# A layer norm over ragged sequences: the first tile's two halves loaded by two engines, the lengths behind one of them

## The chip, the core and the metric

The kernel runs on one core of a Trainium2 chip. A core has five engines with queues of their own: PE (matrix multiply), DVE (vector), ACT (scalar), POOL (GpSimd) and SP (SyncE, which here only issues transfers). SP, ACT and POOL can each start transfers between the main memory (HBM) and the on-chip memory; 16 DMA engines carry them out. The metric is the device time of one execution in microseconds. The kernel before takes 258.73 us (median of three runs, 258.59 to 258.74).

## The reference

```python
batch, max_seq, dim = (32, 512, 1024)
lengths = np.random.randint(64, max_seq, size=batch)
for b in range(batch):
    seq_len = lengths[b]
    x_b = x[b, :seq_len].copy()
    mean = np.mean(x_b, axis=-1, keepdims=True)
    var = np.var(x_b, axis=-1, keepdims=True)
    x_norm = (x_b - mean) / np.sqrt(var + eps)
    output[b, :seq_len] = x_norm * gamma + beta
```

`x` is 64 MB of float32. Rows past a sequence's length come out as zero. Each length is at least 64, so the first 64 rows of every sequence are valid for certain.

## The kernel before

**Tiles.** Four rows of 1024 make a unit of 16 KB; a tile is 128 units, one for each partition, 2 MB. Tiles 0 to 3 are static: they hold the first 64 rows of all 32 sequences, so their addresses do not depend on the lengths. The tiles after them hold the remaining valid rows, packed without holes. Which unit goes where is computed from the lengths: `un` (units in each sequence), `cum` (their running sum), and from these `idx_i`, one column of addresses for each later tile. Units past the lengths are written with zeros from a tile `zt`, 128 units at a time, at addresses `zidx`.

**Transfers.** POOL loads tiles 1 and up with indirect transfers (L556) into eight rotating buffers, stores finished tiles (L578 for tile 0, L585 for the others) and issues the zero stores (L592). Its queue is in program order: load tile 1; some constants; loads of tiles 2 and 3; then, after waiting for `idx_i` and reading the number of units into a register, loads of tiles 4 to 7; the memset of `zt` (L202); then tile after tile a store, a zero store and the load of the tile seven ahead. Tile 0 is loaded directly, without an index, in two halves of 1 MB (two rows for each partition, so 8 KB each), by SP (L531). The half h increments the semaphore `s_xs[h]`. ACT issues at its start the lengths (L519, `len64`, broadcast to all 128 partitions, 256 bytes each), gamma and beta (L520 and L521, into `row_f`).

**Work on a half tile.** The work is done in halves, k = 0, 1, 2, ... DVE takes statistics (L394, four instructions, and L399), ACT a square root (L421), DVE the reciprocal and a small product (L384, L385), ACT the normalisation into float16 (L405), DVE the product with gamma (L378), PE an identity matmul and a matmul that adds beta (L430, L436), and ACT writes the result back into the tile's buffer with a mask as its scale (L414). Then POOL stores the tile.

**Order.** A small scheduler writes each engine's instructions in a fixed order, and an instruction waits only for semaphores. On DVE the order in front is: constants; `lenf` (L231), which waits for the lengths; `rem_i`, `un`, `cum`, `q_f`; the index grid L258 to L267, which ends in `idx_i`; a cast of the identity (L365); and then the statistics of half 0, with this loop:

```python
for k in range(NH):
    if k >= 2:
        dve_mul(k - 2)
    if k >= 1:
        dve_smalls(k - 1)
    dve_stats(k)
    if k == 1:
        tok["maskst"] = mask_static()
```

`mask_static` holds the masks and store addresses of the static tiles, with the cast L294 among them. `zero_index` and `mask_all` follow at k = 3 and k = 5. On ACT the order in front is: its three transfer issues, a table load with a dummy square root (L219), `row_h` (L222, waits for gamma and beta), `gamma_h` (L228), then the square root of half 0. `load_dep(t)` gives the semaphore of a half's data: `s_xs[0]` and `s_xs[1]` for tile 0.

Of the kernel before, what the change touches and what calls it, by code (L numbers as in the profile page):

```python
# [11 lines left out]
P = 128  # L12
UR = 4
ST_ROWS = 64
# [52 lines left out]
def kernel(tc, x, lengths, gamma, beta, eps, out):  # L67
    nc = tc.nc
    B, T, D = x.shape
# [13 lines left out]
    s_len = tc.alloc_semaphore("s_len")  # L83
    s_row = tc.alloc_semaphore("s_row")
    s_xs = [tc.alloc_semaphore(f"s_xs{i}") for i in range(2)]
# [13 lines left out]
    with pool_cm as sb, psum_cm as psb:  # L99
        def st(shape, dt, name):  # L100
            return sb.tile(shape, dt, name=name)

        xt = [st([P, UR * D], FP32, f"x{i}") for i in range(R)]
        ht = [st([P, 2, D], FP16, f"h{i}") for i in range(RH)]
        zt = st([P, UR * D], mybir.dt.bfloat16, "zt")
        len64 = st([P, B], mybir.dt.int64, "len64")
# [71 lines left out]
        def iota(t, pattern, base=0, mult=0):  # L178
# [9 lines left out]
            out=sidx[:, :], in0=p4_i[:, 0:1].broadcast_to([P, NST]), scalar=float(U - S0), in1=sb_i[:, :],  # L188
# [9 lines left out]
            out=idn_f[:, :], in_=idn_f[:, :], compare_op=OP.not_equal, fill=1.0,  # L198
# [141 lines left out]
        def zero_index():  # L340
            n, _, p3 = grid(0, NZ)
            nd = cum[:, B - 1 : B]
            a = add("DVE", lambda: dve.scalar_tensor_tensor(
                out=cz[:, :], in0=cz_f[:, :], scalar=nd, in1=cum[:, :], op0=OP.add, op1=OP.subtract), [a_cz])
            add("DVE", lambda: dve.memset(w3[:, B - 1 : B], 0.0))
            b = add("DVE", lambda: dve.tensor_scalar(out=w3[:, 0 : B - 1], in0=un[:, 1:B], scalar1=float(S0),
                                                     scalar2=None, op0=OP.add))
            z = add("DVE", lambda: dve.scalar_tensor_tensor(
                out=zb[:, :], in0=un[:, 0:1], scalar=float(S0), in1=nd, op0=OP.add, op1=OP.subtract))
            c = add("DVE", lambda: dve.tensor_tensor(  # L350
                out=p3, in0=q_f[:, 0:NZ, None].broadcast_to([P, n, B]),
                in1=cz[:, None, :].broadcast_to([P, n, B]), op=OP.is_ge), [a])
            d = add("DVE", lambda: dve.tensor_tensor(
                out=p3, in0=p3, in1=w3[:, None, :].broadcast_to([P, n, B]), op=OP.mult), [c, b])
            l = add("DVE", lambda: dve.tensor_scalar(out=low[:, :], in0=q_f[:, 0:NZ], scalar1=nd, scalar2=65536.0,
                                                     op0=OP.is_lt, op1=OP.mult))
            e = add("DVE", lambda: dve.tensor_reduce(out=zidx_s[:, :], in_=p3, op=OP.add, axis=AX.X), [d])
            f = add("DVE", lambda: dve.scalar_tensor_tensor(
                out=zidx_f[:, :], in0=q_f[:, 0:NZ], scalar=zb[:, 0:1], in1=zidx_s[:, :], op0=OP.add, op1=OP.add), [e, z])
            return add("DVE", lambda: dve.tensor_tensor(out=zidx[:, :], in0=zidx_f[:, :], in1=low[:, :], op=OP.add),  # L360
                       [f, l])
# [99 lines left out]
        def emit_op(e, name, op):  # L461
            _, fn, waits, inc = op
            for key, val in waits:
                e.wait_ge(handles[key], val)
            ins = fn()
            if inc:
                ins.then_inc(sem[name], 1)

        def units_register(e, name):

            r = e.alloc_register(f"{name}_nd")
            e.wait_ge(sem["DVE"], d_tot[1])
            e.reg_load(r, tot_i[0:1, 0:1])
            return r
# [7 lines left out]
        def run_engine(e, name, block, setup=None):  # L482
            base = nc.cur_bb
            guards = []
            r = None
            if setup is not None:
                setup()
            for op in pr.ops[name]:
                if op[0] == "op":
                    emit_op(e, name, op)  # L490
                else:
                    k = op[1]
                    if k == 2 * NST - 1:
                        r = units_register(e, name)
                        tiles_register(e, r)
                    if k >= 2 * NST + 1 and k % 2 == 1 and k < NH - 1:
                        nxt = f"{name}_s{k + 1}"
                        e.br_lt(r, (k + 1) // 2, f"{name}_exit", nxt)
                        for g in guards:
                            g.__exit__(None, None, None)  # L500
                        guards = [nc.bb(nxt, parent=base)]
                        guards[0].__enter__()
            e.br(f"{name}_exit")
            for g in guards:
                g.__exit__(None, None, None)
            with nc.bb(f"{name}_exit", parent=base):
                e.br(block.end_bb)

        with tc.tile_critical():
            with nc.Block() as block:  # L510

                @block.vector
                def _(e):
                    run_engine(e, "DVE", block)

                @block.scalar
                def _(e):
                    def setup():
                        e.dma_start(out=len64[:, :], in_=lengths[None, :].to_broadcast([P, B])).then_inc(s_len, 16)  # L519
                        e.dma_start(out=row_f[:, 0:D], in_=gamma[None]).then_inc(s_row, 16)  # L520
                        e.dma_start(out=row_f[:, D : 2 * D], in_=beta[None]).then_inc(s_row, 16)  # L521
                    run_engine(e, "ACT", block, setup)
# [4 lines left out]

                @block.sync
                def _(e):
                    for h in range(2):  # L530
                        e.dma_start(out=xt[0][:, 2 * h * D : 2 * h * D + 2 * D],  # L531
                                    in_=x[4 * h : 4 * h + 4, 0:ST_ROWS].rearrange("b (p r) d -> p b (r d)", r=2)
                                    ).then_inc(s_xs[h], 16)
                    e.br(block.end_bb)

                @block.gpsimd
                def _(e):
# [59 lines left out]
                    for op in pr.ops["POOL"]:  # L597
                        if op[0] == "op":
                            emit_op(e, "POOL", op)
                            continue  # L600
                        t = op[1][1]
                        if t == 1:
                            wait(a_sidx)
                        if t == NST:
                            wait(d_idx)
                            rt = units_register(e, "POOL")
                            rb = e.alloc_register("POOL_rb")
                            e.reg_alu(rb, rt, 7, OP.arith_shift_right)
                            tiles_register(e, rt)
                        guarded_load(t)  # L610
# [65 lines left out]
```

## Time and profile before

| what | value |
|---|---|
| median of three runs | 258.73 us |
| the profiled execution | 258.48 us, its span 256.5 us |
| PE, DVE, ACT busy | 141.8, 178.5, 182.9 us |
| POOL busy | 62.2 us |
| HBM read, written | 41.98 MB, 69.21 MB |
| share of the 16 DMA engines: q0 (POOL) | 95.9% |
| the same: q1 (SP), q10 (ACT) | 2.2%, 0.1% |
| packets: q0, q1, q10 | 7632, 288, 148 |

The span runs from the first to the last instruction; the execution's time has some 2 us around it. A line of the timeline has the start and the duration in microseconds, the engine (SPq, ACTq: its queue, here issuing a transfer), the kernel's line, the operation, what is written and what is read, and in brackets how long the engine stood idle before it and what ended that. In the slices of the span each digit is a busy share in tenths. The trace also holds a record of each packet that a DMA engine moved: its start, its queue, its size and its duration.

### The profile page before, as it was taken

How to read it: one execution, taken by the hardware profiler on the slowest of the kernel's cores; microseconds unless marked ns; L12 is line 12 of the kernel's file. 1: busy time of each engine (PE TensorE's matmuls, PEld its weight loads, DVE VectorE, ACT ScalarE, POOL GpSimd, SP SyncE). 2: the span in 40 equal slices, each digit the busy share in tenths (PEclk: the TensorE clock that was granted, in tenths of full speed). 3: DMA queues.
4: the chain of work that ended last, by engine and by line, in shares of the span. 5: the costliest groups of instructions: out<-in, count | busy, mean ns of one | idle time of the engine just before them, and what ended most of it. 6: DMA issues, size and time to landing. Idle time of an engine off the chain costs nothing.

```text
span 256.5 us, 1586 instructions
## 1 busy us (share of the span) xinstructions
PE 141.8 (55%) x306; PEld 32.5 (13%) x306; DVE 178.5 (70%) x421; ACT 182.9 (71%) x198; POOL 62.2 (24%) x68
## 2 busy tenths in 40 slices
PE   0101908274966678668767786677677867820000
PEld 0000202021211111111111111111111111100000
DVE  3979697987688778877887888688868886820000
ACT  2440756758799989998999899989998999850000
POOL 5183021040523322302103402140307130320000
DMA  4999999999999999999999999999999999999980
GB/s 169 426 433 425 432 427 418 436 437 432 425 438 419 441 419 439 427 432 437 424 429 429 432 429 433 422 438 424 439 422 437 416 439 427 432 430 419 442 353 10
DMA packets 8083, 105.42 MB, mean 411 GB/s; under 512 B 1388, under 2 KB 1388, under 8 KB 1390
## 3 DMA queue, kind: packets, MB, share of 16 engines
q0 software_dynamic: 7632, 103.13, 95.9%
q1 hardware_dynamic: 288, 2.10, 2.2%
q8 instruction: 4, 0.07, 0.1%
q14 instruction: 11, 0.09, 0.1%
q10 hardware_dynamic: 148, 0.04, 0.1%
HBM read 41.98 MB, written 69.21 MB: 433 GB/s over the span
## 4 chain that ended last, share of the span: by engine, by line
DVE 35%; PE 28%; ACT 18%; DMA 6%; issue 3%; POOLq 1%; ACTq 1%; SPq 0%; DVEq 0%; POOL 0%
DVE stats_132 L394 18%; PE ps_149 L430 14%; PE ps_149 L436 14%; DMA x_61<-in_x_dram 6%; DVE h_69 L378 3%; DVE h_71 L378 3%; DVE h_70 L378 3%; ACT x_63 L414 3%; ACT x_62 L414 2%; ACT x_61 L414 2%; ACT x_67 L414 2%; ACT x_68 L414 2%; ACT x_66 L414 2%; ACT x_65 L414 2%; ACT x_64 L414 2%
## 5 line engine op out<-in xcount | busy, mean ns | idle before, releaser
L436 PE MATMUL ps_149<-row_h,ones_h 1*128 1x512 f16 x76 | 35.8, 622 | 0.0
L436 PE MATMUL ps_150<-row_h,ones_h 1*128 1x512 f16 x76 | 35.8, 622 | 0.0
L430 PE MATMUL ps_149<-h_69,idn_h 128*128 128x512 f16 x28 | 13.2, 628 | 25.7 <-DVE h_69 L378 25.7
L430 PE MATMUL ps_149<-h_71,idn_h 128*128 128x512 f16 x24 | 11.3, 628 | 15.3 <-DVE h_71 L378 15.3
L430 PE MATMUL ps_149<-h_70,idn_h 128*128 128x512 f16 x24 | 11.3, 627 | 13.7 <-DVE h_70 L378 13.7
L430 PE MATMUL ps_150<-h_70,idn_h 128*128 128x512 f16 x28 | 13.2, 628 | 7.0 <-DVE h_70 L378 7.0
L378 DVE TENSOR_TENSOR h_69<-h_69,gamma_h 128x2048 f16<-128x2048 f16 x13 | 15.5, 1195 | 0.7 <-DVE mv_136 L399 0.7
L592 POOL DMA_INDIRECT out_dram<-zt,zidx x14 | 14.5, 1033 | 5.3 <-issue 4.0
L378 DVE TENSOR_TENSOR h_70<-h_70,gamma_h 128x2048 f16<-128x2048 f16 x13 | 15.4, 1187 | 0.0
L430 PE MATMUL ps_150<-h_71,idn_h 128*128 128x512 f16 x24 | 11.3, 628 | 6.6 <-DVE h_71 L378 6.6
L430 PE MATMUL ps_150<-h_69,idn_h 128*128 128x512 f16 x24 | 11.3, 627 | 6.6 <-DVE h_69 L378 6.6
L378 DVE TENSOR_TENSOR h_71<-h_71,gamma_h 128x2048 f16<-128x2048 f16 x12 | 14.3, 1190 | 0.0
L436 PEld LDWEIGHTS ps_150<-row_h,ones_h 1*128 1x128 f16 x76 | 7.9, 125 | 26.6 <-issue 26.6
L436 PEld LDWEIGHTS ps_149<-row_h,ones_h 1*128 1x128 f16 x76 | 7.9, 125 | 26.6 <-issue 26.6
L384 DVE RECIPROCAL rstd_143<-sq_139 128x2 f32<-128x2 f32 x10 | 1.7, 166 | 13.7 <-ACT sq_139 L421 13.7
L384 DVE RECIPROCAL rstd_141<-sq_137 128x2 f32<-128x2 f32 x10 | 1.7, 166 | 12.6 <-ACT sq_137 L421 12.6
L394 DVE BATCH_NORM_STATS2 stats_132<-x_61 128x6 f32<-128x512 f32 x12 | 7.4, 680 | 1.0 <-DMA x_61<-in_x_dram 1.0
L430 PEld LDWEIGHTS ps_149<-h_69,idn_h 128*128 128x128 f16 x28 | 3.0, 131 | 35.9 <-DVE h_69 L378 32.0
L394 DVE BATCH_NORM_STATS2 stats_131<-x_64 128x6 f32<-128x512 f32 x12 | 7.4, 681 | 0.0
L394 DVE BATCH_NORM_STATS2 stats_132<-x_64 128x6 f32<-128x512 f32 x12 | 7.4, 679 | 0.0
L394 DVE BATCH_NORM_STATS2 stats_131<-x_61 128x6 f32<-128x512 f32 x12 | 7.4, 679 | 0.0
L394 DVE BATCH_NORM_STATS2 stats_132<-x_62 128x6 f32<-128x512 f32 x12 | 7.4, 679 | 0.0
(191 smaller groups left out, 356.6 us busy)
## 6 DMA issues: line engine op xcount, KB each, us to landing
x_61<-in_x_dram SPq DMA_DIRECT2D x2, 1024.0 KB, 7.2
out_dram<-zt,zidx POOLq DMA_INDIRECT x14
len_73<-in_lengths_dram ACTq DMA_DIRECT2D x1, 32.0 KB, 4.3
x_65<-in_x_dram,idx_i POOLq DMA_INDIRECT x2, 20.4
x_66<-in_x_dram,idx_i POOLq DMA_INDIRECT x2, 19.8
x_67<-in_x_dram,idx_i POOLq DMA_INDIRECT x2, 21.6
x_68<-in_x_dram,idx_i POOLq DMA_INDIRECT x2, 23.4
out_dram<-x_61,fidx POOLq DMA_INDIRECT x2, 15.0
```

What stands on the lines that cost most here:

```text
L378: tok["mul", t] = add("DVE", lambda: dve.tensor_tensor(out=h[:, :, :], in0=h[:, :, :], in1=gamma_h[:, None, :].broadcast_to([P, 2, D]), op ...
L384: a = add("DVE", lambda: dve.reciprocal(out=rstd[r][:, :], in_=sq[r][:, :]), [tok["sqrt", t]])
L394: tk = add("DVE", lambda j=j, c=c: dve.bn_stats(out=s[:, j, c, :], in_=xx[:, j * D + c * CH : j * D + c * CH + CH]), [load_dep(t)])
L414: tok["evac", t] = add("ACT", lambda j=j, row=row: act.activation(out=xx[:, j * D : j * D + D], in_=p_[:, j, :], func=AF.Copy, bias=0.0, s ...
L430: add("PE", lambda j=j, c=c: pe.matmul(p_[:, j, c * CH : c * CH + CH], idn_h[:, :], h[:, j, c * CH : c * CH + CH], start=True, stop=False) ...
L436: tok["pe", t] = add("PE", lambda j=j, c=c: pe.matmul(p_[:, j, c * CH : c * CH + CH], ones_h[:, :], row_h[:, D + c * CH : D + c * CH + CH] ...
L592: e.indirect_dma_start(out=ou, out_offset=bass.IndirectOffsetOnAxis(ap=zidx[:, g : g + 1], axis=0), in_=zt[:, :], in_offset=None, bounds_c ...
```

## The change

A helper `first_half(e, h)` issues half h of tile 0 from engine e. SP issues half 0 and then the lengths; ACT issues half 1 and then gamma and beta. Sizes, destinations and semaphores stay as they were, and no other instruction moves on any engine.

```diff
+        def first_half(e, h):
+            e.dma_start(out=xt[0][:, 2 * h * D : 2 * h * D + 2 * D],
+                        in_=x[4 * h : 4 * h + 4, 0:ST_ROWS].rearrange("b (p r) d -> p b (r d)", r=2)
+                        ).then_inc(s_xs[h], 16)
...
                     def setup():
-                        e.dma_start(out=len64[:, :], in_=lengths[None, :].to_broadcast([P, B])).then_inc(s_len, 16)
+                        first_half(e, 1)
                         e.dma_start(out=row_f[:, 0:D], in_=gamma[None]).then_inc(s_row, 16)
                         e.dma_start(out=row_f[:, D : 2 * D], in_=beta[None]).then_inc(s_row, 16)
...
                 def _(e):
-                    for h in range(2):
-                        e.dma_start(out=xt[0][:, 2 * h * D : 2 * h * D + 2 * D],
-                                    in_=x[4 * h : 4 * h + 4, 0:ST_ROWS].rearrange("b (p r) d -> p b (r d)", r=2)
-                                    ).then_inc(s_xs[h], 16)
+                    first_half(e, 0)
+                    e.dma_start(out=len64[:, :], in_=lengths[None, :].to_broadcast([P, B])).then_inc(s_len, 16)
                     e.br(block.end_bb)
```

## The prediction

> **What bounds the kernel now.** I read the page's 40 slices first, then its transfers, the first 25 us of the timeline, and last the chain of waits.
>
> ```profile
> DMA  4999999999999999999999999999999999999980
> GB/s 169 426 433 425 432 427 418 436 437 432 425 438 419 441 419 439 427 432 437 424 429 429 432 429 433 422 438 424 439 422 437 416 439 427 432 430 419 442 353 10
> ```
>
> The DMA engines are full from the second slice on, at about 430 GB/s, and still drain stores after the last compute at 228 us. So the DMA bounds the kernel: its start, its bytes, and any gap. A transfer of 2 MB (one tile) takes about 4.9 us, by the landings of x_65 (13.05 + 17.5) and x_66 (14.35 + 21.1). A compute delay costs only where it opens a gap. The timeline shows where it might (start, duration):
>
> ```profile
> 0.91 0.39 ACTq L519 DMA_DIRECT2D len_73<-in_lengths_dram  x1
> 0.95 1.24 SPq L531 DMA_DIRECT2D x_61<-in_x_dram  x2
> 5.19 0.18 DVE L231 CAST lenf<-len_73 128x32 f32<-128x32 int32 x1 [2.53 <-DMA len_73<-in_lengths_dram]
> 11.27 0.18 DVE L267 CAST idx_i<-idx_f 128x29 int32<-128x29 f32 x1
> 11.50 2.47 DVE L394 BATCH_NORM_STATS2 stats_131<-x_61 128x6 f32<-128x512 f32 x4
> 13.05 0.99 POOL L556 DMA_INDIRECT x_65<-in_x_dram,idx_i  x1 [5.24 <-DVE stats_131 L394]
> 15.97 2.47 DVE L394 BATCH_NORM_STATS2 stats_132<-x_61 128x6 f32<-128x512 f32 x4 [1.04 <-DMA x_61<-in_x_dram]
> 17.93 3.54 POOL L202 MEMSET zt<- 128x4096 bf16 x1
> 19.06 2.43 DVE L294 CAST f_f<-f_i 128x2 f32<-128x2 int32 x1
> 50.72 0.99 POOL L585 DMA_INDIRECT out_dram<-x_62,sidx  x1 [10.83 <-ACT sq_138 L421]
> ```
>
> The lengths release DVE at 5.19. It then works in order to the indices (11.45) and, only behind them, to the statistics of half 0. Half 1 makes DVE wait 1.04 us, until 15.97. From there to 228 us the chain of waits is compute without a wait for a load; its one DMA piece in the front is
>
> ```profile
> 1.61 14.34 DMA x_61<-in_x_dram
> ```
>
> How far the DMA is ahead of the stores is read from issue to landing (last column, us):
>
> ```profile
> out_dram<-x_62,sidx POOLq DMA_INDIRECT x1, 9.1
> out_dram<-x_63,sidx POOLq DMA_INDIRECT x1, 10.4
> out_dram<-x_64,sidx POOLq DMA_INDIRECT x1, 13.7
> ```
>
> Later stores land about 20 us after issue. The store of x_62, issued at 50.72, is the tightest place: POOL's queue is served in order, and counting 128 packets to a transfer in the packet records puts its first packet at 52.98, 2.26 us after issue, with no gap ahead of it. So there is almost no slack there. How queues share an engine is seen in the transfers of 7.2 to 12 us, when POOL's first gather (q0, packets of 16 KB) meets SyncE's second half (q1, 8 KB). The columns are packets, MB, share of 16 engines:
>
> ```profile
> q0 software_dynamic: 87, 1.43, 70.7%
> q1 hardware_dynamic: 88, 0.62, 32.3%
> ```
>
> Equal packets, not equal bytes: they take turns. A 16 KB packet takes 0.611 us and an 8 KB one 0.309 in the records.
>
> [...] the cast at 19.06 ends at 21.49 with the memset (21.47).
>
> **The change, part by part.** *Issue.* SyncE still issues two transfers (half 0, lengths), ScalarE still three (half 1, gamma, beta). Half 1 is issued 0.64 us earlier (0.91 for 1.55), the lengths 0.64 later. DVE, PE and POOL keep their order. ScalarE issues an x transfer of 0.6 us for one of 0.39, and its table load moves by about 0.2 us: hidden, its next work waited 3.33 us for gamma and beta.
>
> *DMA start.* Until now the lengths went first on every engine: their packets start at 1.93 and the first x packet follows the last of them on each (2.40 to 4.83). Gain: the lead of 0.47 us; from below 0, if the x data cannot come before 3.8 anyway (eight first packets end there wherever they started), and above 1.9: the windows from 2 to 6 us moved 0.9 MB where 430 GB/s gives 1.72. I take 0.5. It counts only if no gap comes later.
>
> *The lengths' landing, L.* This decides. They stand on SyncE's ring behind the 8 packets of half 0 on each engine, and these now take turns with the 8 of half 1 on ScalarE's ring, from 7.2 us also with POOL's packets. An engine that ends its first x packet at 3.8 has ended 12 of 16 by 7.2 (3.4 / 0.309 = 11 more). The last two pairs take 2 × (0.309 + 0.309 + 0.611) = 2.46, to 9.66. Then come half 0's completion packet, 8 rows of lengths and their completion packet. If each takes a turn, each waits for a 16 KB packet: 10 × 0.62 = 6.2, to 15.9; with 0.36 from last packet to DVE (4.83 to 5.19) L = 16.2. Bounds: if the rows go in one turn, 9.66 + 2 × 0.62 + 0.36 = 11.3; if the slowest engine is as late as now (first x packet ends at 5.68, POOL's packets there from 7.85), 8 are left of each pair's 16, 4 rounds of 1.23, and L = 7.85 + 4.9 + 6.2 + 0.36 = 19.3. I take separate turns, because even 4-byte completion packets wait for their own turn in the records (half 1: data to 14.61, a 16 KB packet, completion at 15.22).
>
> *What is queued behind.* DVE: 6.3 us of index work, the statistics of half 0, everything. The 1.04 us wait for half 1 goes (it lands by 14), but what is late next is the cast at L294: POOL's memset comes after the four indexed gathers, which hang on L too, ends at L + 16.28, and holds the cast up to that point. So from there compute moves by the whole L − 5.19 = 11.0. Gamma and beta land on the engine of ScalarE's ring behind half 1, at about 12.5; with 1.91 + 1.03 + 1.02 us of work ScalarE is free at 16.6, before its first square root at L + 9.05 = 25: hidden, and in the way only if L were under 7.6.
>
> *The gap.* POOL's x_65 goes out at L + 7.86 = 24.1. The first four tiles run out near 24, so a gap of about 2 us opens there; but the store of x_62 sets the sum. It is issued at 50.72 + 11.0 = 61.7. Its start latency on an empty queue is not in the trace: at most 2.26 us, at least its own issue, 0.99. [...] The first packet is then at 63.7 for 52.98: the end moves by L − 5.19 − 0.27 = **10.7 us**. This holds the gap near 24 and swallows the 0.5 us won. The next store comes 13.5 us later, with three transfers of 4.9 ahead: no new gap, and no return, since the DMA is full to the end. 258.48 + 10.7 = 269.2; the median of the runs stands 0.25 over the profiled execution: **269.4**.
>
> **Rivals.** (a) One turn: the lengths' eight rows drain as one packet. L 11.3 to 14.4, the end moves by 5.8 to 8.9: 264.5 to 267.6. For: [...] no x packet stands between the lengths' rows and their completion now. Against: completion packets waiting alone. (b) Half 0 first: its packets are not slowed by half 1; it is through by 7.8 as now, and L is about 9: +3.5, 262.2. For: half 0 landed 7.2 us after issue with half 1 behind it. Against: the equal turns of 7.2 to 12 us. (c) Faster: the start is won and the store of x_62 is not late. Needs L under 5.46, where the gap term turns zero; then 258.7 − 0.5 = 258.2, and 256.8 if all of the 1.9 us is won. For: the end is set by the DMA, and the DMA starts earlier. Against: half 0 alone needs 8 × 0.309 = 2.5 us on an engine after 3.8.
>
> **How the numbers follow.** Separate turns 0.53 (267.5 to 272.6), one turn 0.30, half 0 first 0.10, faster 0.03, no change 0.01, later than 272.6 0.03. A range of 263.8 to 272.0 leaves under 2 in 10 out. A measurement here tells 0.2%, 0.5 us, from no change: faster 0.03, same 0.01, slower 0.96.
>
> **What would show it.** In the changed profile L231 starts at 16, with its wait put down to the lengths; L294 still ends with the memset; x_61 lands earlier in its second half, by 14; POOL's store of x_62 is near 61.7; two slices, near 24 and 58 us, lose DMA share. L231 near 11 means one turn, near 9 half 0 first. It is wrong if L231 is late and no slice loses share: the queue then had more ahead than I counted.

## The result and the profile after

The changed kernel takes 269.08 us (median of six runs, four of them from 268.99 to 269.87, two at 266.27 and 266.36) where the kernel before takes 258.70 us (258.59 to 258.83) beside it: 1.0374 times as long, with a 95% interval of 1.0317 to 1.0432. The profiled execution took 268.99 us, its span is 267.0 us: 10.5 us more than the 258.48 and 256.5 us of before.

The slices of the span, as on the page of the changed kernel (6.7 us each, DMA share in tenths and GB/s):

```profile
DMA  6997999954999999999999999999999999999990
GB/s 263 364 385 287 392 430 400 417 211 196 432 431 432 431 431 427 432 432 432 432 432 425 432 432 432 426 427 428 430 430 427 432 430 430 434 426 423 433 378 29
```

From the eleventh slice on it is the old picture: a full DMA. What is new lies in front. The first slice moves more (263 for 169 GB/s), then come three places with less: the second and third slice, the fourth, and the ninth and tenth. The timeline of the same kernel names them (start, duration):

```profile
0.92 0.66 ACTq L470 DMA_DIRECT2D x_61<-in_x_dram  x1
1.64 0.83 SPq L536 DMA_DIRECT2D len_73<-in_lengths_dram  x1
16.70 0.18 DVE L231 CAST lenf<-len_73 128x32 f32<-128x32 int32 x1 [14.04 <-DMA len_73<-in_lengths_dram]
24.50 0.99 POOL L559 DMA_INDIRECT x_65<-in_x_dram,idx_i  x1 [16.68 <-DVE stats_131 L394]
29.36 3.53 POOL L202 MEMSET zt<- 128x4096 bf16 x1
29.37 3.55 DVE L294 CAST f_f<-f_i 128x2 f32<-128x2 int32 x1
62.14 0.99 POOL L588 DMA_INDIRECT out_dram<-x_62,sidx  x1 [10.84 <-ACT sq_138 L421]
```

DVE waits 14.04 us for the lengths and starts at 16.70, 11.51 us later than before. The first gather that needs the indices leaves at 24.50 for 13.05, and the store of x_62 at 62.14 for 50.72: 11.42 us later. The chain of waits in front has turned from a transfer of x into one of the lengths:

```profile
1.64 15.03 DMA len_73<-in_lengths_dram
```

The gaps stand in the windows of the changed kernel; the last two columns are DMA share and GB/s:

```profile
10.00:12.00 2.00, 0.62 (x2) 0.00 (x0) 0.00 (x0) 1.02 (x1) 0.00 (x0) 1.00 0.80 300
12.00:14.00 2.00, 0.00 (x0) 0.00 (x0) 0.00 (x0) 0.00 (x0) 0.00 (x0) 1.00 0.68 251
24.00:26.00 2.00, 0.00 (x0) 0.00 (x0) 1.66 (x5) 0.30 (x1) 1.20 (x2) 1.00 0.04 16
58.00:63.00 5.00, 0.18 (x1) 0.00 (x0) 4.85 (x14) 3.53 (x5) 0.86 (x1) 1.00 0.00 0
63.00:64.00 1.00, 0.00 (x0) 0.00 (x0) 1.00 (x2) 0.00 (x0) 0.69 (x2) 1.00 0.62 262
```

Five full microseconds without a byte, while DVE and ACT work on the tile that POOL is to store. By the packet records the store's first packet is at 63.70, against 52.98 before: 10.72 us later, and the whole execution is 10.51 us longer. Only 0.2 us are won back behind that point.

Why the lengths are so late is seen in the transfers from 9.3 to 15.7 us of the changed kernel (packets, MB, share of the 16 engines):

```profile
q0 software_dynamic: 138, 2.00, 81.0%
q1 hardware_dynamic: 137, 0.03, 2.0%
```

q1 has the rows of the lengths now, 256 bytes each, and 4-byte packets, of which the lengths have 16 at their end (completion packets: DVE starts 0.36 us after the last of these, 16.34 to 16.70); q0 has the 16 KB rows of POOL's gather. 138 packets against 137: they take turns, one for one.

### The profile page after: what moved, and what is told of

It is laid out like the page before. It is cut to its first block, busy times and chain, and to the rows that moved or that the text cites. A ratio compares the mean times of both kernels' runs of the same rounds, so it can differ in the third digit from the quotient of the medians.

```text
span 267.0 us, 1586 instructions
## 1 busy us (share of the span) xinstructions
PE 141.7 (53%) x306; PEld 32.4 (12%) x306; DVE 179.5 (67%) x421; ACT 182.9 (68%) x198; POOL 64.6 (24%) x68
## 4 chain that ended last, share of the span: by engine, by line
DVE 37%; PE 26%; ACT 17%; DMA 6%; issue 3%; POOLq 0%; ACTq 0%; SPq 0%; DVEq 0%; POOL 0%
DVE stats_132 L394 17%; PE ps_149 L430 13%; PE ps_149 L436 13%; DMA len_73<-in_lengths_dram 6%; DVE h_69 L378 3%; DVE h_71 L378 3%; DVE h_70 L378 3%; ACT x_63 L414 2%; ACT x_62 L414 2%; ACT x_61 L414 2%; ACT x_66 L414 2%; ACT x_68 L414 2%; ACT x_67 L414 2%; ACT x_64 L414 2%; ACT x_65 L414 2%
## 5 line engine op out<-in xcount | busy, mean ns | idle before, releaser
L595 POOL DMA_INDIRECT out_dram<-zt,zidx x14 | 15.2, 1088 | 5.3 <-issue 4.0
L421 ACT ACTIVATE sq_137<-mv_133,eps_sb 128x2 f32<-128x2 f32 x10 | 2.9, 293 | 14.0 <-DVE mv_133 L399 14.0
L559 POOL DMA_INDIRECT x_65<-in_x_dram,idx_i x2 | 2.6, 1284 | 22.5 <-DVE stats_131 L394 16.7
L394 DVE BATCH_NORM_STATS2 stats_132<-x_63 128x6 f32<-128x512 f32 x12 | 7.4, 680 | 0.0
L394 DVE BATCH_NORM_STATS2 stats_131<-x_62 128x6 f32<-128x512 f32 x12 | 7.4, 680 | 0.0
## 6 DMA issues: line engine op xcount, KB each, us to landing
x_68<-in_x_dram,idx_i POOLq DMA_INDIRECT x2, 19.5
```

What stands on the lines that cost most here:

```text
L394: tk = add("DVE", lambda j=j, c=c: dve.bn_stats(out=s[:, j, c, :], in_=xx[:, j * D + c * CH : j * D + c * CH + CH]), [load_dep(t)])
L421: tok["sqrt", t] = add("ACT", lambda: act.activation(out=sq[r][:, :], in_=mv[r][:, :, 1], func=AF.Sqrt, bias=eps_sb[:, 0:1], scale=1.0), [ ...
L559: e.indirect_dma_start(out=xt[t % R][:, :], out_offset=None, in_=xu, in_offset=bass.IndirectOffsetOnAxis(ap=column(t), axis=0), bounds_che ...
L595: e.indirect_dma_start(out=ou, out_offset=bass.IndirectOffsetOnAxis(ap=zidx[:, g : g + 1], axis=0), in_=zt[:, :], in_offset=None, bounds_c ...
```

## The experiments

Most are read at one number, the issue of the store of x_62, and at the time. The theory: the lengths' rows each take a turn beside a full queue, which the recorded texts call a ring; that delays DVE; the delay moves the store of x_62, and from there a late store is an idle DMA.

**1. The lengths first on SyncE, the halves still on two engines.**

```diff
-                    first_half(e, 0)
                     e.dma_start(out=len64[:, :], in_=lengths[None, :].to_broadcast([P, B])).then_inc(s_len, 16)
+                    first_half(e, 0)
```

> Split halves kept, lengths put first on SyncE. Theory (the late lengths cost it all): the lengths release DVE near 5.5 us, the store of tile 1 is issued near 51 us, no gap in the DMA after the start, 257.5 to 259.5 us. Rival (loading the halves by two engines costs by itself, through contention at the start): DVE starts early but the time stays over 262 us.

Measured: 258.67 us, 1.0002 times the kernel before (0.9993 to 1.0011). DVE has the lengths at 5.94:

```profile
5.94 0.18 DVE L231 CAST lenf<-len 128x32 f32<-128x32 int32 x1 [3.28 <-DMA len<-in_lengths_dram]
```

The store is issued at 52.06, 1 us later than expected and 1.34 later than before, and the medians do not differ (the two profiled executions differ by 0.3 us). So loading the halves by two engines is free when the lengths come first; the loss comes with their place behind half 0. It also shows the edge of the slack: of 1.3 us of lateness at the store at least 1.0 is hidden.

**2. Only the lengths moved, behind half 0; both halves on SyncE.**

```diff
                     def setup():
-                        e.dma_start(out=len64[:, :], in_=lengths[None, :].to_broadcast([P, B])).then_inc(s_len, 16)
...
                 def _(e):
-                    for h in range(2):
-                        e.dma_start(out=xt[0][:, 2 * h * D : 2 * h * D + 2 * D],
-                                    in_=x[4 * h : 4 * h + 4, 0:ST_ROWS].rearrange("b (p r) d -> p b (r d)", r=2)
-                                    ).then_inc(s_xs[h], 16)
+                    first_half(e, 0)
+                    e.dma_start(out=len64[:, :], in_=lengths[None, :].to_broadcast([P, B])).then_inc(s_len, 16)
+                    first_half(e, 1)
```

> Only the lengths are moved: SyncE issues half 0, lengths, half 1, as the kernel before otherwise. Theory (each small row waits for its turn beside a full ring of 16 KB packets): half 0 is alone on its engine until 7.2 us, so the lengths' rows pass before the gather's packets come on most engines; DVE is released at 8.5 to 10 us and the end moves by 2.5 to 4.5 us, to 261 to 263 us. Rival (standing behind 1 MB on a ring is the whole cost, whoever else is there): DVE is released near 16 us and the time is near 269 us, as in the changed kernel.

Measured: 260.2 us, 1.0062 (1.0045 to 1.0078). DVE is released at 7.86 and the store issued at 53.29:

```profile
7.86 0.18 DVE L231 CAST lenf<-len 128x32 f32<-128x32 int32 x1 [5.19 <-DMA len<-in_lengths_dram]
```

Both came out below the expected ranges: the direction held, the delay was less than thought. Standing behind 1 MB of the same queue, that of one issuing engine, cost 2.7 us of DVE's start here, not 11.5. In this run the gather's first packet came at 8.72, after the last row of the lengths (7.53): what the rows meet beside them decides.

**3. No large packet beside the rows.** The changed kernel, with POOL's first gather held back until the lengths are there:

```diff
                         if t == 1:
                             wait(a_sidx)
+                            wait(("len", 16))
```

> The changed kernel, but POOL's first gather waits until the lengths have landed, so no 16 KB packet stands beside their rows. Theory (turns): the lengths land at 9 to 10 us instead of 16.7 although they stand where they stood; a gap of some 4 us opens behind them because the gather starts late, and the store of tile 1 is no longer late: about 263 us (262 to 265). Rival (the rows themselves are slow behind 2 MB, or their reads of one address are): the lengths land after 13 us still, and with the late gather the time is over 269 us.

Measured: 263.63 us, 1.0189 (1.0172 to 1.0206). The lengths stand where the change put them, behind half 0 and with half 1 on the other queue, and are there 8 us sooner:

```profile
8.68 0.18 DVE L231 CAST lenf<-len 128x32 f32<-128x32 int32 x1 [6.01 <-DMA len<-in_lengths_dram]
```

In the packet records the 128 rows start from 7.63 to 8.31, in 0.7 us; in the changed kernel from 9.29 to 15.72. This is the theory's sharpest point, and the rival (the rows are slow by themselves) falls. What the time still loses is the gather's own late start; windows of this run:

```profile
8.00:10.00 2.00, 0.27 (x1) 0.12 (x2) 1.15 (x8) 1.68 (x1) 0.35 (x1) 1.00 0.04 8
10.00:12.00 2.00, 0.76 (x2) 0.00 (x0) 1.01 (x5) 1.02 (x1) 1.82 (x8) 1.00 0.52 115
```

**4. The lengths twice.** The changed kernel, SyncE loading the lengths first into a tile that nothing reads, then as before: nine packets more on every engine.

```diff
+    s_len_d = tc.alloc_semaphore("s_len_d")
...
+        len_d = st([P, B], mybir.dt.int64, "len_d")
...
                     first_half(e, 0)
+                    e.dma_start(out=len_d[:, :], in_=lengths[None, :].to_broadcast([P, B])).then_inc(s_len_d, 16)
                     e.dma_start(out=len64[:, :], in_=lengths[None, :].to_broadcast([P, B])).then_inc(s_len, 16)
```

> The changed kernel with the lengths loaded twice on SyncE, first into a tile that nothing reads. Theory (each row and completion packet takes a turn of 0.62 us): nine more turns, the lengths land 5.6 us later (22.3 us) and the time rises by as much, to 274.5 us (273.5 to 275.5). Rival (the eight rows of a ring drain in one turn): at most 1.3 us later, 269 to 270.5 us. If a delay of DVE were partly hidden, the time would rise by less than the landing does.

Measured: 274.56 us, 1.0613 (1.0595 to 1.0631). DVE starts at 22.27, and the store is issued at 67.71:

```profile
22.27 0.18 DVE L233 CAST lenf<-len 128x32 f32<-128x32 int32 x1 [19.61 <-DMA len<-in_lengths_dram]
```

Both are 5.57 us later than in the profile of the changed kernel, and 5.0 us later than in its second profile (experiment 8). The packet records of this run itself are more exact. The completion packets of the first load start at 15.44 to 16.86 us, those of the second at 20.43 to 21.85: in order of time, each of the 16 is 4.98 us after its counterpart. That is eight turns of 0.62 us, one 16 KB packet each (0.611 us in the records). By the count, one of the nine packets of 256 or 4 bytes on each engine passed beside the gather's own completion packet (4 bytes, 19.2 to 19.5 us), which takes 0.009 us in the changed kernel's records, and cost next to nothing. So the forecast of 22.3 was met with one turn fewer than it counted, because the first load was 0.5 us later here than in the profile of the changed kernel (16.86 for 16.34). The rival of one turn for all rows (at most 1.3 us) falls. And the time rises with it, by 5.5 us over the changed kernel's first runs (269.08) and 5.0 over its later ones (269.56): nothing of a delay is hidden any more.

**5. and 6. The lengths as one row.** If 128 small rows cost ahead of the tile as well, one row of 256 bytes should be better than both kernels. ScalarE loads it first; PE spreads it to 128 partitions with a matmul of ones. Run 6 also moves POOL's memset of `zt` ahead of its wait for the indices.

```diff
-        len64 = st([P, B], mybir.dt.int64, "len64")
+        len64 = st([1, B], mybir.dt.int64, "len64")
+        len_h = st([1, B], FP16, "len_h")
...
+        d_lh = add("DVE", lambda: dve.tensor_copy(out=len_h[:, :], in_=len64.bitcast(INT32)[:, 0::2]), [("len", 16)])
+        e_len = add("PE", lambda: pe.matmul(ps[1][:, 0, 0:B], ones_h[:, :], len_h[:, :], start=True, stop=True),
+                    [d_lh, d_one])
...
-        d_len = add("DVE", lambda: dve.tensor_copy(out=lenf[:, :], in_=len64.bitcast(INT32)[:, 0::2]), [("len", 16)])
+        d_len = add("DVE", lambda: dve.tensor_copy(out=lenf[:, :], in_=ps[1][:, 0, 0:B]), [e_len])
...
                     def setup():
+                        e.dma_start(out=len64[:, :], in_=lengths[None, :]).then_inc(s_len, 16)
                         first_half(e, 1)
...
                     first_half(e, 0)
-                    e.dma_start(out=len64[:, :], in_=lengths[None, :].to_broadcast([P, B])).then_inc(s_len, 16)
```

> Halves on two engines, and the lengths as one row of 256 B, first on ScalarE, spread to 128 partitions by a matmul with ones. Theory (what cost time was 128 small rows, ahead of the tile in the kernel before, behind it in the changed one): DVE has the lengths by 5 us, the DMA moves x at full rate from about 2.4 us, 1.3 us earlier than before; the store of tile 1 is issued near 50.5 us and is almost the bound, so 257.4 to 258.2 us. Rival (an earlier DMA start is lost again later): 258.7 us.

> As the run with one row, and POOL's memset of the zero tile placed ahead of its wait for the indices, so that the cast L294 is not held by it. Theory: the compute chain is another 2.4 us ahead, the store of tile 1 is issued near 48 us, the whole early start of the DMA is kept: 257.2 to 257.6 us. Rival (early start lost later): 258.7 us.

Measured: 259.10 us, 1.0017 (1.0009 to 1.0024), and 259.18 us, 1.0023 (1.0017 to 1.0030). Both expectations failed, and the rival was still too kind. The store of x_62 was issued at 49.70 and 49.94, so run 6 gained nothing by its early memset: there it held two other casts, L272 and L370, for 1.9 and 1.8 us. The start came as expected: `lenf` is written at 3.02 and the windows of run 5 from 2 to 4 us have 279 GB/s, where the kernel before has 87. First run 5:

```profile
2.00:4.00 2.00, 0.20 (x1) 0.10 (x1) 1.57 (x10) 1.07 (x1) 1.36 (x3) 1.00 0.84 279
40.00:45.00 5.00, 4.72 (x11) 1.16 (x11) 2.82 (x8) 3.45 (x5) 0.00 (x0) 1.00 0.97 351
250.00:251.00 1.00, 0.00 (x0) 0.00 (x0) 0.00 (x0) 0.00 (x0) 0.00 (x0) 1.00 0.13 49
252.00:253.00 1.00, 0.00 (x0) 0.00 (x0) 0.00 (x0) 0.00 (x0) 0.00 (x0) 1.00 0.08 33
```

The same stretches of the kernel before:

```profile
2.00:4.00 2.00, 0.00 (x0) 0.00 (x0) 0.59 (x6) 1.58 (x2) 1.36 (x3) 1.00 0.39 87
40.00:45.00 5.00, 4.72 (x12) 1.03 (x11) 3.01 (x6) 3.88 (x5) 0.00 (x0) 1.00 0.97 408
252.00:253.00 1.00, 0.00 (x0) 0.00 (x0) 0.00 (x0) 0.00 (x0) 0.00 (x0) 1.00 0.00 0
```

The gain is lost in two places. From 40 to 45 us, where the queue turns from loads to stores, the share is 0.97 as before, but only 351 GB/s move (before: 408; run 6: 339). Those are 0.29 MB, 0.7 us of the 1.1 us lead that it had at 24 us by the sum of the packet records. And at the end a tail of few packets lasts longer. In the kernel before POOL's last packet ends at 252.37 and the span at 256.55; in run 5 at 253.46 and 257.62, in run 6 at 253.01 and 257.23: the span ends 4.2 us after the last packet in all three. The last four packets of run 5 end at 251.64, 252.24, 252.85 and 253.46, one after the other, 0.60 to 0.61 us apart, as on one engine that works alone. In these runs the end follows the last packet to finish, not the mean of all engines. (The profiled execution of run 5, 259.68 us, is its slowest; that of run 6, 259.24, is near its median and shows the same.) Why the turn from loads to stores is slower with an early start, and why one engine is left behind, was not settled.

**7. The memset earlier in the kernel before**, nothing else.

```diff
         for t in range(2, R):
+            if t == NST:
+                a_zt = add("POOL", lambda: pool.memset(zt[:, :], 0.0))
             pr.raw("POOL", ("load", t))
-        a_zt = add("POOL", lambda: pool.memset(zt[:, :], 0.0))
```

> The kernel before with POOL's memset of the zero tile ahead of its wait for the indices, nothing else. Theory (the DMA is full, compute has slack of under 1 us at the store of tile 1 and otherwise only follows): the store of tile 1 is issued 2.2 to 2.4 us earlier, near 48.4 us, and the time stays within 0.2% of 258.7 us. Rival (compute bounds the kernel): 256.3 us.

Measured: 258.58 us, 1.0004 (0.9990 to 1.0018). The time is as expected, but not for the reason given: the store is issued at 51.45, not 48.4. The memset now holds another instruction, on the way to the indices:

```profile
7.66 3.73 DVE L246 TENSOR_SCALAR t_f<-t_f,tb_f 128x29 f32<-128x29 f32 x1
7.83 3.53 POOL L202 MEMSET zt<- 128x4096 bf16 x1
```

So whether compute alone would gain was not tried; that 0.7 us of lateness at the store is free agrees with experiment 1.

**8. The changed kernel again**, for its spread.

> The changed kernel once more, for its spread: 266.3 to 269.9 us as before. If the spread comes from the lengths' landing, a run with a shorter time has an earlier L231 by as much (14 us for 266.3 us); if from elsewhere, L231 stays at 16.7 us.

Measured: 269.56 us (269.50 to 269.77), 1.0424 (1.0408 to 1.0439). The profile has DVE at 17.27 and the store at 62.70, both 0.6 us later than in the first one, and the execution is 0.5 us longer. None of these four runs was near 266.3, where two of the six before had been, so the cause of those two stays open.

**9. The memset earlier in the changed kernel**, by the same edit as in 7. Here DVE stands idle while the memset runs.

> The changed kernel with POOL's memset of the zero tile ahead of its wait for the indices, where POOL and DVE both stand idle. Theory (the memset held the cast L294 and passed the whole lateness of the lengths on; the store of tile 1 sets the end): L231 stays at 16.7 to 17.3 us, the cast takes 0.2 us instead of 3.55, the store of tile 1 is issued 3.4 us earlier (58.7 to 59.3 us), and the time falls by as much, to 265.6 to 266.2 us. Rival (the gap near 24 us, ahead of the indexed gathers, costs by itself, since they still leave at the same time): the time stays at 268 us or more.

Measured: 266.24 us, 1.0290 (1.0273 to 1.0308): 2.8 us less than the changed kernel's median, 3.3 less than in experiment 8. DVE starts at 16.73, and the cast is short:

```profile
29.41 0.17 DVE L295 CAST f_f<-f_i 128x2 f32<-128x2 int32 x1
58.80 0.99 POOL L589 DMA_INDIRECT out_dram<-x,sidx  x1 [10.83 <-ACT sq L422]
```

The gap ahead of the indexed gathers is there as before (DMA share 0.00 from 24 to 26 us), so it costs nothing while the store is later still: what follows it only waits less at the store.

Side by side, each from the profiled execution:

| kernel | DVE gets the lengths | store of x_62 issued | execution, us | execution less issue |
|---|---|---|---|---|
| before | 5.19 | 50.72 | 258.48 | 207.8 |
| 1, lengths first | 5.94 | 52.06 | 258.79 | 206.7 |
| 2, behind half 0 | 7.86 | 53.29 | 260.19 | 206.9 |
| 3, gather held | 8.68 | 55.03 | 263.61 | 208.6 |
| 9, changed, memset early | 16.73 | 58.80 | 265.47 | 206.7 |
| changed | 16.70 | 62.14 | 268.99 | 206.9 |
| 8, changed again | 17.27 | 62.70 | 269.50 | 206.8 |
| 4, lengths twice | 22.27 | 67.71 | 274.47 | 206.8 |

Where the store is the bound, the execution ends 206.7 to 206.9 us after its issue, for issues from 52.06 to 67.71. In the kernel before and in experiment 3 it ends later than that, because there the DMA and not the store is late: in experiment 3 the store's first packet comes 1.83 us after its issue, behind a full queue, where an empty one takes 1.55 to 1.58 (the other rows).

## Why the prediction was right, step by step

**The bound** was read rightly: a full DMA, hidden compute, and one tight place, the store of x_62. The table shows it, and experiment 1 its slack. The prediction left a slack of 0.27 us, the 2.26 us from issue to first packet less a start latency that the author assumed and no trace of before showed. The latency measured in the changed kernel is 1.56, which leaves 0.7, and by the table's last column it is 1.0 (207.8 less 206.8).

**The landing of the lengths** was forecast at 16.2 and came at 16.70 (17.27 in the second profile). Separate turns were right, on the evidence named, the completion packets that waited alone: 138 to 137 packets here, and eight turns of 0.62 us in experiment 4. But two terms on the way were wrong, and it is luck that they nearly cancel. The prediction let the two halves take turns from the start. They did not: by the packet records ScalarE's half 1 ran alone from 2.35, SyncE's first packet came at 4.67, and half 1 had started its last packet at 5.38 and half 0 at 8.79. So half 0's completion packets, forecast at 10.3, came at 8.98 in the mean of the 16 engines (8.67 to 9.87). The nine turns after them, eight rows and a completion, were forecast at 5.6 us and took 6.7 in the mean (to 15.70), and the slowest engine ended at 16.34. No engine was as late as the one that gave the 19.3 us bound.

**What is queued behind** held: the cast at L294 starts 0.01 us after the memset and ends with it, and the 1.04 us that half 1 used to cost bring nothing. Experiment 9 takes the memset away: the store comes 3.34 us earlier, as long as the cast was held (3.55 for 0.17), and the execution is 3.5 us shorter. Gamma and beta were hidden, and landed earlier than forecast (L222 at 7.63 for about 12.5), since they stood behind half 1, which had no company until 4.67.

**The gap** was forecast with a first packet 2.0 us after the store's issue (61.7 to 63.7). That was the author's assumption: the trace of before bounds it at 2.26 from above and does not show it. Measured it was shorter: the store's first packet came 1.56 us after issue (62.14 to 63.70). The issue was 0.4 us later than forecast (62.14 for 61.7), so the first packet came at 63.7, as forecast: here too two misses cancel. The gap near 24 us was there and was swallowed by the later one.

**The DMA's start** was sized too low: 0.5 us, where the windows from 2 to 6 us moved 1.47 MB for 0.90, and 0.57 MB at 430 GB/s are 1.3 us. The prediction had kept open whether x data can come before 3.8 us; it can. It made no difference: from 10 to 14 us the share fell to 0.80 and 0.68 while the rows of the lengths were under way, by 24 us the changed kernel had moved 8.45 MB for 8.65 before, and the gaps came after. Experiments 5 and 6 show that this gain is not even kept where no gap comes.

**The rivals.** One turn: experiments 3 and 4 rule it out. Half 0 first: half of it came true, as half 1 was first, and it saved nothing because the rows met the gather. Faster: experiment 1 shows that the split without late lengths is no gain either.

## What to carry to other kernels

A short transfer that the program waits for should not stand behind bulk on its queue, and less so while another queue holds large packets: behind 1 MB the 32 KB of the lengths reached DVE 2.7 us later (experiment 2), with 16 KB packets beside them 11.5 us later. Count its packets for each engine, and give each the time of the packet that it takes turns with (here 0.62 us for 16 KB), not its bytes. In a kernel with a full DMA, look for the first store that comes close to an empty queue: here at least 1.0 us of its lateness was free (experiment 1), and beyond that 5.57 us of lateness were 5.5 us of time (experiment 4 against the changed kernel). A transfer moved behind another moves all that waits for it, here two engines in program order and four gathers.

## What the runs showed of the hardware that was not expected

- While the rows of the lengths took turns with the gather, the engines were not always busy: from 9.3 to 15.7 us of the changed kernel the share of both queues is 83%. That is not a price of small packets as such. In experiment 4, from 15.7 to 20 us, 127 small packets take turns with 126 of POOL's queue and the share is 101%:

```profile
q0 software_dynamic: 126, 1.80, 97.9%
q1 hardware_dynamic: 127, 0.03, 3.2%
```

  What left engines idle before that stays open.
- Two transfers of 128 rows of 8 KB, issued at almost the same time by SyncE (0.95) and ScalarE (0.92), did not start together: first packets at 4.67 and 2.35. By 4.67, 112 of ScalarE's 128 packets had started. In experiment 2 the rows of the lengths, with no other packet beside them, took from 5.21 to 7.53, 2.3 us too, and the engines were all but idle; here the transfers from 5.2 to 7 us of that run:

```profile
DMA packets 127, 0.04 MB, mean 25 GB/s; under 512 B 125, under 2 KB 125, under 8 KB 125
```

  The cause of these 2.3 us was not shown: in experiment 3 the same rows passed in 0.7 us, and in the kernel before the first x packet (2.40) came while rows of the lengths, issued before it, went on until 4.81. No run was made for this alone, and it stays open.
- A memset of POOL held not only casts but also a DVE instruction of another kind, TENSOR_SCALAR (3.73 us instead of 0.24, experiment 7; it ended at 11.39, the memset at 11.36).
